# A transformer encoder layer: the first feed-forward product as seven half-size products, its result kept in DRAM, and the second product as a phase of its own

## The chip, the cores and the metric

The kernel runs on one core of one Trainium2 chip. The time is the device time of one execution in microseconds (us); a kernel's time is the median of its runs. One execution of each kernel is also recorded by the hardware profiler, and all durations of single instructions come from that one. The engines are named as in the profile: PE is TensorE (PEld its weight load), DVE VectorE, ACT ScalarE, POOL GpSimd, SP SyncE, which here issues the DMAs.

## The reference

Two inputs, 256 and 1024 tokens of 1024 channels, go through the same encoder layer: a norm, one wide projection, four mixers, a gated merge, an output projection with residual, and a feed-forward part with residual. Cut to the last two, which the change touches:

```python
merged = sum over n of gate[:, :, n] * einsum('blw,wd->bld', branches[n], w_branch[n])
mix_out = einsum('bld,de->ble', merged, w_out)          # 1024 x 1024
x = x + rms_norm(mix_out, norm_mix_post)
h2 = rms_norm(x, norm_ffn_pre)
hidden = square(relu(einsum('bld,df->blf', h2, w_ff1)))  # 1024 x 4096
ff_out = einsum('blf,fd->bld', hidden, w_ff2)            # 4096 x 1024
return x + rms_norm(ff_out, norm_ffn_post)
```

All is float32.

## The kernel before

The 1280 tokens are ten tiles of 128 (`NT`), taken together in chunks of 256, 512 and 512 tokens (`CH`). Every large product is made from three TensorE products: each operand is split into a high part, rounded to the multiplier's float32 form, and a low part that holds the rest, and `PASSES` adds high by high, high by low and low by high in PSUM. Weights come in units of 128 x 512 floats, 256 KB. `wload` loads a unit on SP's queue into one of three raw buffers (L112), casts the high part on ACT (L116) and subtracts it on DVE for the low part (L117); high and low parts lie in a ring of 16 tiles "w".

After the merge, `split` makes the high and low part of a token tile (L973 and L974), the output projection multiplies it with both halves of the output weights, first one half over all of K and then the other (`gemm_b`, L153), and `residual` adds the normed result to the input, stores it, and makes the normed `h2` tile in place of the merged one (L989 to L1002), with two small powers on POOL (L106). `transpose_in` turns each `h2` tile with eight TensorE transposes (L194) into high and low parts (L196 on ACT, L197 on DVE).

In the feed-forward part, `ffn1(f)` makes 128 hidden channels for all tokens: three chunks of 24 matmuls (8 K tiles by 3 passes, `gemm_a`, L146) with 256 or 512 columns, then relu, square and the high part on ACT (L1034 to L1036) and the low part on DVE (L1037). `ffn2(fs)` then multiplies two such hidden blocks with their two weight units and adds the result of every token tile to an accumulator in SBUF (L1058 on TensorE, L1064 on DVE): 15 rounds of 120 to 180 matmuls after a first one. `ffn1` runs up to three hidden blocks ahead. In the last round, `finish` makes the last norm and the output (L1068 to L1090). The order on TensorE from the output projection to `ffn1(0)` is that of the code (`manual_schedule`); elsewhere, and on the other engines, a scheduler sets it from the code's order and the buffers. Each engine works through its own list in order, and an instruction waits for what it reads and for the last use of the buffer that it writes.

## Time and profile before

| | |
|---|---|
| median of 3 runs | 2324.14 us (2323.52 to 2324.39) |
| span of the profiled execution | 2322.2 us |
| from the output projection's first matmul to the first product's | 1307.05 to 1429.24 us |
| feed-forward part | 1429.24 to 2312.64 us (end of the last matmul) |
| after the last matmul | 9.56 us |
| mean granted TensorE clock | 0.997 |

The profiler counts from the first to the last instruction of one execution, so its span is 1.9 us below the median of the runs. Rows of a group read: line, engine, operation, output<-input by the program's names, shapes, count | busy time, mean duration of one in ns | idle time ahead of them and what ended it. A busy TensorE includes overlap of one matmul with the next, so the distance between starts, not the duration of one, tells the pace. Rows of the chain and of a timeline begin with start and duration in us. Rows of a table by stretches give the stretch, its length, the busy time and count of instructions of each engine named (TensorE alone, or TensorE, its weight load, DVE, ACT and POOL), the granted clock, the DMA share and GB/s.

### The profile page before, as it was taken

Reading aid. Unit: us, or ns where it says so; the run is one execution under the profiler, and the core shown is the slowest. Engines: PE = TensorE matmul, PEld = TensorE weight load, DVE = VectorE, ACT = ScalarE, POOL = GpSimd, SP = SyncE. Lnnn points to the kernel's source line nnn. Section 1 sums busy time; section 2 is a strip of 40 time slices with the busy share of each in tenths; the row PEclk is TensorE's granted clock in tenths of the full one; section 3 lists DMA queues with packets and bytes.
Section 4 is the critical chain, followed back from the end, with each engine's and each line's share of the span. In section 5 each row is a group of like instructions: output and inputs, shape, how many; then the busy total and the mean of one; then the engine's idle time right before and its main releaser. Section 6 shows DMA issues by size and latency. Waiting matters only on the chain.

```text
span 2322.2 us, 29598 instructions
## 1 busy us (share of the span) xinstructions
PE 2288.3 (99%) x11680; PEld 1931.8 (83%) x11680; DVE 1084.1 (47%) x1757; ACT 751.8 (32%) x1514; POOL 65.1 (3%) x126
## 2 busy tenths in 40 slices
PE   8999999999999999999999999999999999999998
PEld 6887888878888888888888788888888888888886
DVE  5465599677554332322422455244444444334437
ACT  5333886334332121211211234422222222222223
POOL 1000000000000000000000011000000000000001
PEclk9999999999999999999999999999999999999999
DMA  5212565634276320210211423111111111111104
GB/s 178 77 41 104 177 215 163 200 101 143 87 249 214 120 68 28 82 46 28 96 32 36 137 91 127 37 37 37 37 37 37 37 41 47 40 37 39 43 24 163
DMA packets 117516, 205.22 MB, mean 88 GB/s; under 512 B 11105, under 2 KB 41985, under 8 KB 117377
## 3 DMA queue, kind: packets, MB, share of 16 engines
q1 hardware_dynamic: 107584, 187.60, 25.7%
q10 hardware_dynamic: 9792, 15.73, 1.9%
q8 instruction: 91, 1.49, 0.3%
q14 instruction: 49, 0.39, 0.1%
HBM read 153.40 MB, written 49.89 MB: 88 GB/s over the span
## 4 chain that ended last, share of the span: by engine, by line
PE 92%; DVE 4%; DMA 1%; issue 1%; ACT 1%; POOL 0%; SPq 0%; DVEq 0%; POOLq 0%; ACTq 0%
PE mm L146 47%; PE mm L1058 17%; PE mm L244 11%; PE mm L153 6%; PE mm L251 6%; PE mx L584 1%; DMA raw<-in_wu_dram 1%; DVE acc L1089 1%; PE mx L194 1%; DVE sa L715 0%; DVE acc L1064 0%; PE mx L470 0%; PE mx L595 0%; PE mx L827 0%; PE mx L864 0%
## 5 line engine op out<-in xcount | busy, mean ns | idle before, releaser
L146 PE MATMUL mm<-h2T,whi 128*128 128x512 f32 (+1 forms) x1536 | 408.0, 354 | 0.3 <-ACT h2T L196 0.3
L146 PE MATMUL mm<-hT,whi 128*128 128x256 f32 (+1 forms) x1488 | 395.5, 354 | 0.0
L117 DVE TENSOR_TENSOR wlo<-raw,whi 128x512 fp32r<-128x512 f32 x302 | 206.7, 689 | 373.0 <-ACT whi L116 318.6
L116 ACT CAST whi<-raw 128x512 fp32r<-128x512 f32 x302 | 184.5, 621 | 581.1 <-PE mm L1058 320.5
L146 PEld LDWEIGHTS mm<-h2T,whi 128*128 128x128 f32 x1536 | 271.8, 189 | 40.9 <-ACT h2T L196 0.5
L146 PEld LDWEIGHTS mm<-hT,whi 128*128 128x128 f32 x1488 | 263.4, 189 | 38.9
L1064 DVE TENSOR_TENSOR acc<-acc,mm 128x512 f32<-128x512 f32 x300 | 205.7, 686 | 154.7 <-PE mm L1058 154.7
L146 PE MATMUL mm<-h2T,wlo 128*128 128x512 f32 (+1 forms) x768 | 271.5, 354 | 0.0
L146 PE MATMUL mm<-hT,wlo 128*128 128x256 f32 (+1 forms) x744 | 263.1, 354 | 0.0
L244 PE MATMUL mm<-hT,whi 128*128 128x512 f32 (+1 forms) x960 | 261.4, 360 | 0.0
L1058 PE MATMUL mm<-whi,hidl 128*128 128x512 f32 x640 | 251.1, 392 | 0.0
L1058 PE MATMUL mm<-whi,hidh 128*128 128x512 f32 x640 | 250.2, 391 | 0.0
L1058 PE MATMUL mm<-wlo,hidh 128*128 128x512 f32 x640 | 248.5, 388 | 0.0
L146 PE MATMUL mm<-bt,whi 128*128 128x512 f32 (+1 forms) x768 | 204.3, 354 | 0.0
L244 PEld LDWEIGHTS mm<-hT,whi 128*128 128x128 f32 x960 | 166.9, 189 | 26.4 <-issue 3.3
L244 PE MATMUL mm<-hT,wlo 128*128 128x512 f32 (+1 forms) x480 | 170.2, 355 | 0.0
L1037 DVE TENSOR_TENSOR hidl<-relu,hidh 128x512 fp32r<-128x512 f32 (+1 forms) x96 | 57.9, 603 | 238.8 <-ACT hidh L1036 238.8
L146 PEld LDWEIGHTS mm<-h2T,wlo 128*128 128x128 f32 x768 | 145.1, 189 | 20.2
L146 PEld LDWEIGHTS mm<-hT,wlo 128*128 128x128 f32 x744 | 140.6, 189 | 19.6
L146 PEld LDWEIGHTS mm<-bt,whi 128*128 128x128 f32 x768 | 136.0, 189 | 20.5
L251 PE MATMUL mm<-whi,hT 128*128 128x512 f32 x480 | 151.8, 397 | 0.0
L1058 PEld LDWEIGHTS mm<-whi,hidh 128*128 128x128 f32 x640 | 120.1, 188 | 27.0
(259 smaller groups left out, 2824.0 us busy)
## 6 DMA issues: line engine op xcount, KB each, us to landing
raw<-in_wu_dram SPq DMA_DIRECT2D x310, 256.0 KB, 2.7
E<-acsd SPq DMA_DIRECT2D x20, 512.0 KB, 4.8
bt<-br SPq DMA_DIRECT2D x16, 640.0 KB, 6.1
br<-bo SPq DMA_DIRECT2D x36, 256.0 KB, 3.0
xt<-in_x_dram SPq DMA_DIRECT2D x10, 512.0 KB, 3.8
oxt<-in_x_dram SPq DMA_DIRECT2D x10, 512.0 KB, 3.6
x2d<-oxt SPq DMA_DIRECT2D x10, 512.0 KB, 2.6
fx<-x2d SPq DMA_DIRECT2D x10, 512.0 KB, 3.9
```

Of the source, the lines that this page charges most:

```text
L116: ACT.copy(out=hi, in_=raw)
L117: DVE.tensor_tensor(out=lo, in0=raw, in1=hi.bitcast(F32), op=ALU.subtract)
L146: PE.matmul(ps[:, :n], w.get(a, k), act.rhs(b, k, c), start=j == 0, stop=j == last)
L153: PE.matmul(ps, act.lhs(b, k, t), w.get(a, k), start=j == 0, stop=j == last)
L194: PE.transpose(tp[:, i * 128:(i + 1) * 128], src[:, k, :], ident)
L244: yield from halves(ps, w, n, lambda ps, w, a, b, k, st, sp: PE.matmul(ps[:, :n], w.get(a, k), hT.rhs(b, k, c), start=st, stop=sp))
L251: yield from halves(ps, w, 512, lambda ps, w, a, b, k, st, sp: PE.matmul(ps, hT.lhs(b, k, t), w.get(a, k), start=st, stop=sp))
L584: PE.matmul(yd[:, 64 * h:64 * h + 64], E[:, 128 * h:128 * h + 128], xs[:, 64 * h:64 * h + 64], start=True, stop=True)
L1037: DVE.tensor_tensor(out=hl[:, c0:c0 + n], in0=r[:, :n], in1=hh[:, c0:c0 + n].bitcast(F32), op=ALU.subtract)
L1058: PE.matmul(ps, hid[f][p][:, 128 * t:128 * t + 128], ws[i][e][a], start=j == 0, stop=j == end)
L1064: DVE.tensor_tensor(out=dst, in0=dst, in1=ps, op=ALU.add)
L1089: DVE.scalar_tensor_tensor(out=a, in0=a, scalar=rs, in1=xt[:, cols], op0=ALU.mult, op1=ALU.add)
```

## The change

The first product, `h2` (1280 x 1024) by 1024 x 4096, is cut for each pair of hidden blocks q (256 channels; 16 pairs) into halves in all three directions: the tokens in even and odd tiles (A1x and A2x), K in two halves of 512, the channels in two halves of 128. Seven products of half size take the place of eight, in Winograd's form of Strassen's scheme: `LEFT` lists sums and differences of the token halves, T1 to T4 are differences of weight units, and the four results are sums of the products. P1, P6, P7 and P4 go one after the other into one PSUM bank "a" without a restart, P2 into "c", P5 and P3 into "d". ACT copies the bank out after P1, P6 and P7 (L1157); DVE adds the bank c or d to such a copy and takes relu and square (L1160 to L1175, L1145); P4's result goes through ACT (L1170, L1171). Each product is 12 matmuls (4 K tiles by 3 passes, L1153).

The five pairs of token tiles form a group of two pairs (c = 0, 256 columns) and one of three (c = 1, 384 columns). `build` makes the left operands of one tile pair: 16 transposes (L999), eight operations on ACT and eleven on DVE (L1004 to L1019). The first two pairs are built during the output projection; the other three `h2` pairs are stored to DRAM and read back. There are three phases: for q = 0 to 5 the narrow group alone (with a build after q = 1, 2 and 4), for q = 6 to 15 both groups, and for q = 0 to 5 the wide group alone, with the weights loaded and combined again. So `ff1_w` runs 22 times: four raw loads, four differences (on POOL for the first phase, else on DVE, L1106), seven casts on ACT (L1100) and seven subtractions on DVE (L1101).

The hidden values are stored to DRAM in float32 (L1141) and read back tile by tile in the second product (`load_h`, L1251, with cast and subtraction at L1254 and L1255), which is a phase of its own: eight rounds over K by ten token tiles, each with 24 matmuls of 512 columns (L1277). The accumulator is added to 140 times, not 300. The output projection now takes both halves of the weights at each K tile (L1067), and `split` works on half tiles. The table pools change place, and the code's order on TensorE (`manual_schedule`) now holds to the end.

```diff
+LEFT = ("A11", "A12", "S2", "S1", "S3", "A22", "S4")
+PRODUCTS = (("P1", "A11", "B11", "a"), ("P2", "A12", "B21", "c"), ("P6", "S2", "T2", "a"), ("P5", "S1", "T1", "d"),
+            ("P7", "S3", "T3", "a"), ("P4", "A22", "T4", "a"), ("P3", "S4", "B22", "d"))
+CP = (2, 3)
+HN = (256, 384)
+NQ0 = 6
+BUILD_AT = (1, 2, 4)
...
+    def left(p, c):
+        return {o: [p.tile([128, 4, HN[c]], F32R, name=f"{o}{c}{b}") for b in range(2)] for o in reversed(LEFT)}
+    AL = [left(ap0, 0), None]
+    def ts():
+        return tp.tile([128, 512], F32, tag="ts", name="ts", bufs=3)
 
     def k4(a):
         return a.rearrange("p (k b) -> p k b", b=128)
 
+    def build(p, even, odd):
+        c = 0 if p < CP[0] else 1
+        o = 128 * (p - c * CP[0])
+        def tr(src, g):
+            ps = mx_ps()
+            for i in range(4):
+                PE.transpose(ps[:, i * 128:(i + 1) * 128], src[:, 4 * g + i, :], ident)
+            return ps
+        def put(name, a):
+            hi, lo = (AL[c][name][b][:, :, o:o + 128] for b in range(2))
+            ACT.copy(out=hi, in_=k4(a))
+            DVE.tensor_tensor(out=lo, in0=k4(a), in1=hi.bitcast(F32), op=ALU.subtract)
+        a21, a22, a11, a12 = tr(odd, 0), tr(odd, 1), tr(even, 0), tr(even, 1)
+        x = ts()
+        ACT.copy(out=x, in_=a21)
+        s1 = ts()
+        DVE.tensor_tensor(out=s1, in0=x, in1=a22, op=ALU.add)
+        DVE.tensor_tensor(out=x, in0=a11, in1=x, op=ALU.subtract)
+        put("A22", a22)
+        put("S1", s1)
+        DVE.tensor_tensor(out=s1, in0=s1, in1=a11, op=ALU.subtract)
+        put("A11", a11)
+        put("S3", x)
+        s4 = ts()
+        DVE.tensor_tensor(out=s4, in0=a12, in1=s1, op=ALU.subtract)
+        put("A12", a12)
+        put("S2", s1)
+        put("S4", s4)
...
+        if t >= 2 * CP[0]:
+            SP.dma_start(out=k4(h2d[t]), in_=ht)
...
-        for half in range(2):
-            gemm_b(ps[half], w[half], act, t)
+        for k in range(8):
+            for half in range(2):
+                for i, (a, b) in enumerate(PASSES):
+                    PE.matmul(ps[half], act[k // 4][b][:, k % 4, :], w[half].get(a, k), start=k + i == 0,
+                              stop=k == 7 and i == 2)
         act = nact
         pend.append(residual(t, ps))
-        if 1 <= t <= CT[2][0]:
-            transpose_in(h2T, pend[t - 1], t - 1)
...
+    hid = [dram.tile([NT, 128, 512], F32, name=f"hid{i}") for i in range(DFF // 512)]
...
+    def ff1_w(q, eng):
+        r = {}
+        for name, f, g in (("B11", 0, 0), ("B21", 0, 1), ("B12", 1, 0), ("B22", 1, 1)):
+            if name == "B12":
+                raw = tp.tile([128, 512], F32, tag="raw", name="raw", bufs=1)
+            else:
+                raw = wp.tile([128, 512], F32, tag="raw", name="raw", bufs=3)
+            SP.dma_start(out=raw, in_=wu[FF1_U + 4 * q + 2 * f + g])
+            r[name] = raw
+        out = {}
+        def put(name, a):
+            hi = wp.tile([128, 512], F32R, tag="w", name="whi", bufs=16)
+            lo = wp.tile([128, 512], F32R, tag="w", name="wlo", bufs=16)
+            ACT.copy(out=hi, in_=a)
+            DVE.tensor_tensor(out=lo, in0=a, in1=hi.bitcast(F32), op=ALU.subtract)
+            out[name] = hi, lo
+        def diff(a, b):
+            d = ts()
+            eng.tensor_tensor(out=d, in0=a, in1=b, op=ALU.subtract)
+            return d
+        put("B11", r["B11"])
+        put("B21", r["B21"])
+        t1 = diff(r["B12"], r["B11"])
+        t2 = diff(r["B22"], t1)
+        put("T2", t2)
+        put("T1", t1)
+        t4 = diff(r["B21"], t2)
+        t3 = diff(r["B22"], r["B12"])
+        put("T3", t3)
+        put("T4", t4)
+        put("B22", r["B22"])
+        return out
+    def ff1(q, w, cs, fc):
+        bank = {}
+        tiles = {}
+        def new(c, nm):
+            tiles[c, nm] = fc[c].tile([128, HN[c]], F32, tag=f"fc{c}", name=f"fc{c}", bufs=6 + c)
+            return tiles[c, nm]
+        def ps_of(b, c):
+            if (b, c) not in bank:
+                bank[b, c] = (mm_ps if b == "a" or len(cs) == 1 else mx_ps)()
+                return bank[b, c][:, :HN[c]], True
+            return bank[b, c][:, :HN[c]], False
+        def done(c, nm, half, fo):
+            f = 2 * q + fo
+            dst = hid[f // 4].rearrange("(a b) p c -> b p a c", b=2)[half]
+            o = c * CP[0]
+            SP.dma_start(out=dst[:, o:o + CP[c], 128 * (f % 4):128 * (f % 4) + 128],
+                         in_=tiles[c, nm].rearrange("p (a b) -> p a b", b=128))
+        def relu2(a):
+            DVE.scalar_tensor_tensor(out=a, in0=a, scalar=0.0, in1=a, op0=ALU.max, op1=ALU.mult)
+        for name, lo, ro, b in PRODUCTS:
+            for c in cs:
+                ps, first = ps_of(b, c)
+                j = 0
+                for k in range(4):
+                    for a, p in PASSES:
+                        PE.matmul(ps, w[ro][a][:, 128 * k:128 * k + 128], AL[c][lo][p][:, k, :], start=first and j == 0,
+                                  stop=j == 11, skip_group_check=not first)
+                        j += 1
+                if name in ("P1", "P6", "P7"):
+                    ACT.copy(out=new(c, name), in_=ps)
+                if name == "P2":
+                    s = tiles[c, "P1"]
+                    DVE.tensor_tensor(out=s, in0=s, in1=ps, op=ALU.add)
+                    relu2(s)
+                    done(c, "P1", 0, 0)
+                if name == "P7":
+                    s = tiles[c, "P7"]
+                    DVE.tensor_tensor(out=s, in0=s, in1=bank["d", c][:, :HN[c]], op=ALU.add)
+                    relu2(s)
+                    done(c, "P7", 1, 1)
+                if name == "P4":
+                    s = new(c, "P4")
+                    ACT.activation(out=s, in_=ps, func=AF.Relu)
+                    ACT.activation(out=s, in_=s, func=AF.Square)
+                    done(c, "P4", 1, 0)
+                if name == "P3":
+                    s = tiles[c, "P6"]
+                    DVE.tensor_tensor(out=s, in0=s, in1=ps, op=ALU.add)
+                    relu2(s)
+                    done(c, "P6", 0, 1)
+    NQ = DFF // 256
+    fc = [fc0, None]
+    wq = ff1_w(0, POOL)
+    for q in range(NQ0):
+        nw = ff1_w(q + 1, POOL)
+        ff1(q, wq, (0,), fc)
+        wq = nw
+        if q in BUILD_AT:
+            p = CP[0] + BUILD_AT.index(q)
+            src = []
+            for t in (2 * p, 2 * p + 1):
+                h = hst.tile([128, 8, 128], F32, name="hst", bufs=2)
+                SP.dma_start(out=h, in_=k4(h2d[t]))
+                src.append(h)
+            build(p, *src)
+    hst.release()
+    fc[1] = pool("fc1", side="right")
+    for q in range(NQ0, NQ):
+        nw = ff1_w((q + 1) % NQ, DVE)
+        ff1(q, wq, (0, 1), fc)
+        wq = nw
+    ap0.release()
+    w2p = pool("w2")
+    for q in range(NQ0):
+        nw = ff1_w(q + 1, DVE) if q + 1 < NQ0 else None
+        ff1(q, wq, (1,), fc)
+        wq = nw
...
+    fin = {}
+    units = [0]
+    def ff2_w(kc):
+        ws = {}
+        for e in range(2):
+            for fo in range(4):
+                raw = wp.tile([128, 512], F32, tag="raw", name="raw", bufs=3)
+                SP.dma_start(out=raw, in_=wu[FF2_U + 2 * (4 * kc + fo) + e])
+                pl, tag, nb = (wp, "w", 16) if units[0] % 22 < 8 else (w2p, "w2", 28)
+                units[0] += 1
+                hi = pl.tile([128, 512], F32R, tag=tag, name="whi", bufs=nb)
+                lo = pl.tile([128, 512], F32R, tag=tag, name="wlo", bufs=nb)
+                ACT.copy(out=hi, in_=raw)
+                DVE.tensor_tensor(out=lo, in0=raw, in1=hi.bitcast(F32), op=ALU.subtract)
+                ws[e, fo] = hi, lo
+        return ws
 
...
+    def load_h(kc, t):
+        raw = fp.tile([128, 512], F32, name="hraw", bufs=3)
+        SP.dma_start(out=raw, in_=hid[kc][t])
+        hh = fp.tile([128, 512], F32R, name="hidh", bufs=3)
+        hl = fp.tile([128, 512], F32R, name="hidl", bufs=3)
+        ACT.copy(out=hh, in_=raw)
+        DVE.tensor_tensor(out=hl, in0=raw, in1=hh.bitcast(F32), op=ALU.subtract)
+        return hh, hl
+    NK = DFF // 512
+    kcs = [(i + (NQ0 + 1) // 2) % NK for i in range(NK)]
+    steps = [(i, t) for i in range(NK) for t in range(NT)]
+    ws = ff2_w(kcs[0])
+    nws = None
+    hs = [load_h(kcs[0], 0), load_h(kcs[0], 1)]
+    for n, (i, t) in enumerate(steps):
+        if t == 0 and i:
+            ws = nws
+        if t == 1 and i + 1 < NK:
+            nws = ff2_w(kcs[i + 1])
+        if n + 2 < len(steps):
+            hs.append(load_h(kcs[steps[n + 2][0]], steps[n + 2][1]))
+        h = hs.pop(0)
+        last = i == NK - 1
+        for e in range(2):
+            ps = mm_ps()
+            for fo in range(4):
+                for m, (a, p) in enumerate(PASSES):
+                    PE.matmul(ps, h[p][:, 128 * fo:128 * fo + 128], ws[e, fo][a], start=fo + m == 0,
+                              stop=fo == 3 and m == 2)
...
+    finish(NT - 1)
+    order.close()```

Three places show how the lists of the engines change. In the names, a number behind a tile's name tells one buffer from another; what an instruction waits for stands in brackets.

On ACT in the first product before, the end of one hidden block with the weight casts that follow; `mm` is the PSUM bank of a chunk:

```order
L1034 ACTIVATE relu_13220<-mm_13195 128x512 [waits DVE_49,PE_49]
L1035 ACTIVATE relu_13220<-relu_13220 128x512 [waits Activation_49]
L1036 CAST hidh_13133<-relu_13220 128x512 [waits Activation_49]
L116 CAST whi_13619<-raw_13617 128x512 [waits DMAHW4_49,PE_49]
L116 CAST whi_13625<-raw_13623 128x512 [waits DMAHW5_49,PE_49]
```

On ACT now, in the first phase at q = 1; `mm_12176` is bank a, `fc0` are the copies (P1, P6, P7) and P4's tile, and `whi` are the weights of q = 2: B11, B21, T2, T1, T3, T4 and B22 in this order:

```order
L1157 COPY fc0_12189<-mm_12176 128x256 [waits PE_49]
L1100 CAST whi_12152<-ts_12150 128x512 [waits PE_49,Pool_49]
L1100 CAST whi_12156<-ts_12148 128x512 [waits DVE_49,PE_49]
L1157 COPY fc0_12219<-mm_12176 128x256 [waits PE_49]
L1100 CAST whi_12164<-ts_12162 128x512 [waits PE_49,Pool_49]
L1100 CAST whi_12168<-ts_12160 128x512 [waits DVE_49,PE_49]
L1157 COPY fc0_12246<-mm_12176 128x256 [waits DMAHW7_49,PE_49]
L1100 CAST whi_12172<-raw_12138 128x512 [waits DMAHW5_49,DVE_49,PE_49]
L1170 ACTIVATE fc0_12263<-mm_12176 128x256 [waits DMAHW3_49,DVE_49,PE_49]
L1171 ACTIVATE fc0_12263<-fc0_12263 128x256 [waits Activation_49]
```

Where ACT read a bank once and then worked in SBUF, it now reads the same bank four times, with the casts of the next pair's weights between; the casts of T3 (`whi_12164`) and T4 (`whi_12168`) stand ahead of P7's copy (`fc0_12246`). The ring "w" has eight pairs of high and low tiles for seven operands, so an operand of q = 2 takes the place of the one before it in the list of q = 1: T4 that of T3, which P7 reads.

On DVE now, at the start of the build that follows q = 1; `mx` are the transposed tiles, `ts` the sums, and `A..`, `S..` the left operands:

```order
L1101 TENSOR_TENSOR wlo_12337<-raw_12328,whi_12336 128x512 [waits DMAHW7_49,Activation_49]
L1011 TENSOR_TENSOR ts_12308<-ts_12306,mx_12291 128x512 [waits PE_49,Activation_49]
L1012 TENSOR_TENSOR ts_12306<-mx_12296,ts_12306 128x512 [waits DVE_49,PE_49]
L1005 TENSOR_TENSOR A2211_11921<-mx_12291,A2210_11920 128x4x128 [waits Activation_49]
L1005 TENSOR_TENSOR S111_11925<-ts_12308,S110_11924 128x4x128 [waits DMAHW3_49,DMAHW6_49,DMAHW1_49,Activation_49]
L1005 TENSOR_TENSOR S311_11923<-ts_12306,S310_11922 128x4x128 [waits Activation_49]
L1015 TENSOR_TENSOR ts_12308<-ts_12308,mx_12296 128x512 [waits DVE_49]
L1101 TENSOR_TENSOR wlo_12341<-raw_12330,whi_12340 128x512 [waits DMAHW1_49,PE_49,Activation_49]
```

The build's operations stand among the low parts of the weights of the pair after next; there was nothing of the kind in the first product before.

On SP now, where the first product ends and the second begins; `fc1` are the wide group's hidden tiles, `hraw` the hidden values read back:

```order
L1141 DMA hid2_11909<-fc1_16408 128x3x128 [waits DVE_49]
L1223 DMA raw_16562<-in_wu_dram 128x512 [waits DMAHW6_49,DMAHW2_49,DVE_49]
L1141 DMA hid2_11909<-fc1_16425 128x3x128 [waits Activation_49]
L1214 DMA gfin_16460<-in_rows_dram 128x1024 [waits PE_49]
L1141 DMA hid2_11909<-fc1_16381 128x3x128 [waits DMAHW5_49,DVE_49]
L1251 DMA hraw_16510<-hid3_11910 128x512
L1251 DMA hraw_16516<-hid3_11910 128x512 [waits DMAHW7_49]
```

The store of the last hidden tile (`fc1_16381`, made after P3) waits for DVE, and the loads for the second product, of another 512 channels (`hid3`), stand behind it on the same queue. Before, hidden values never left SBUF and SP had only weights to load here.

124 lines of the change are left out of this document (46 added, 78 removed).

## The prediction

> **What bounds the kernel now.** I read the page first: busy shares, the chain by engine and line, the costly groups.
>
> ```profile
> span 2322.2 us, 29598 instructions
> PE 2288.3 (99%) x11680; PEld 1931.8 (83%) x11680; DVE 1084.1 (47%) x1757; ACT 751.8 (32%) x1514; POOL 65.1 (3%) x126
> PE 92%; DVE 4%; DMA 1%; issue 1%; ACT 1%; POOL 0%; SPq 0%; DVEq 0%; POOLq 0%; ACTq 0%
> raw<-in_wu_dram SPq DMA_DIRECT2D x310, 256.0 KB, 2.7
> ```
>
> TensorE is busy for 99% of the span and makes 92% of the chain; nothing else is above half. The profiled execution spans 2322.2 us and the median of the runs is 2324.1, so I add 1.9 us to a span to compare it with the runs. Next, what TensorE waits for:
>
> ```profile
> PE mm L153 <- ACT wout L116: 4.4, 2, 3.3
> PE mx L194 <- DVE h2T L197: 1.6, 1, 1.6
> PE mm L146 <- ACT h2T L196: 0.3, 1, 0.3
> ```
>
> In the feed-forward part only the last two, 1.9 us together, belong to its start; from there on TensorE never waits. The chain of waits in that part and a table by stretches give the pace:
>
> ```profile
> 1502.40 27.47 PE mm L1058 x120
> 1529.87 27.56 PE mm L146 x144
> 1557.43 27.33 PE mm L1058 x120
> ...
> 1196.07:1198.94 2.87, 2.87 (x25) 1.00 0.28 96
> 1198.94:1209.85 10.91, 10.91 (x51) 1.00 0.15 48
> ```
>
> The pieces alternate: 144 matmuls of the first product (L146, two hidden blocks) and 120 of the second (L1058). The two stretches are one 256-column chunk of 24 matmuls and two 512-column chunks, 48 matmuls (the counts also hold those that straddle an edge). So a 256-column matmul takes 2.87/24 = 119.6 ns, a 512-column one 10.91/48 = 227.3 ns, and 48 x 119.6 + 96 x 227.3 = 27.56 us, just the piece of the chain. The clock column is 1.00. Time can only leave by fewer column-passes, and whatever makes TensorE wait comes on top.
>
> **The change: matmuls.** Before, the first product is 16 pieces of 27.56 = 441.0 us. After, each of 16 column pairs has seven products of 12 matmuls: 84 of 256 columns and 84 of 384. No row has 384 columns. Three quarters of 227.3 is 170.5; one and a half times 119.6 is 179.4; the straight line between both widths gives 173.4, which I take, since both known widths lie on one line with a fixed part of 12 ns. 84 x 119.6 = 10.05 us, 84 x 173.4 = 14.57 us, together 24.6; 16 x 24.6 = 393.8. **Gain 47.2 us** (39 to 51). The second product keeps its 1920 matmuls of 512 columns: 0. Transposes are 80 before and after: 0.  The 1.9 us wait at the start of the first product goes, since the first group's left operands are built six tiles earlier.
>
> **What is added on DVE, ACT and the DMAs.** Prices, by shape, and last two stretches, of 16 transposes and of the whole feed-forward part:
>
> ```profile
> L117 DVE TENSOR_TENSOR wlo<-raw,whi 128x512 fp32r<-128x512 f32 x302 | 206.7, 689 | 373.0 <-ACT whi L116 318.6 <-PE mm L146 37.7 <-PE mm L244 9.4
> L948 DVE SCALAR_TENSOR_TENSOR gth<-gth,mm 128x256 f32<-128x256 f32 x24 | 10.0, 418 | 106.5 <-PE mm L146 106.5
> L1064 DVE TENSOR_TENSOR acc<-acc,mm 128x512 f32<-128x512 f32 x300 | 205.7, 686 | 154.7 <-PE mm L1058 154.7
> L116 ACT CAST whi<-raw 128x512 fp32r<-128x512 f32 x302 | 184.5, 621 | 581.1 <-PE mm L1058 320.5 <-PE mm L146 127.0 <-DMA raw<-in_wu_dram 86.4
> L909 ACT ACTIVATE gth<-mm 128x256 f32<-128x256 f32 x24 | 9.2, 383 | 99.2 <-PE mm L146 98.4 <-issue 0.8
> L648 POOL MEMSET reset<- 128x1280 f32 x1 | 1.2, 1167 | 0.0
> ...
> 1427.58 1.91 PE L194 MATMUL mx<-cst,merged 128*128 128x128 f32 x16
> 1429.24 0.48 PE L146 MATMUL mm<-h2T,whi 128*128 128x256 f32 x2
> ...
> 1427.58:2322.20 894.62, 883.15 (x4257) 744.12 (x4255) 376.32 (x592) 259.70 (x482) 10.30 (x12) 1.00 0.16 49
> ```
>
> One column pair needs on DVE seven subtractions for low parts (7 x 0.69 = 4.8 us) and six 256-wide operations on the hidden tiles (6 x 0.42 = 2.5 us): 7.3 us, against 10.05 us of matmuls in the first phase, where only the 256-column group runs. A pair with a build has 11 more DVE operations (11 x 0.69 = 7.6): 14.9, against 10.05 + 1.7 for its transposes (1429.24 - 1427.58). Over the six pairs of that phase DVE has 6 x 7.3 + 3 x 7.6 = 67 us for 65 of TensorE: level with it, so order decides.
>
> The weight differences run on POOL there, four a pair. The nearest POOL row, one access per element, is 1167/1280 = 0.91 ns; three accesses to 512 elements are 1.4 us, the upper bound; DVE's 0.69 for the same operation the lower. I take 1.2, nearer POOL's own row: 4.8 us a pair beside 10. The Trainium skill, "GPSIMD Engine Reference", section 3.1, puts a two-input operation at about 2.6 cycles an element, by which I estimate 1.1 us; nothing in the sum changes.
>
> The hidden values are 1280 x 4096 x 4 = 21 MB, written once and read once. With the DMAs 16% busy at 49 GB/s there, 42 MB more over 850 us are 49 GB/s more, about a third busy in all: 0, under the matmuls. Not so covered, at the mean rate of the whole span (88 GB/s), they would take 42/0.088 = 477 us; the stores in pieces of 512 bytes have no row here.
>
> **Waits in the first phase.** The fourth product in bank a goes on accumulating P1, P6 and P7, so P4 cannot start until ACT has copied P7 out. In ACT's list the cast of T4 stands ahead of that copy, and this cast overwrites the slot that P7 reads: it cannot start before P7 ends. How fast ACT takes over:
>
> ```profile
> 1281.54 0.28 PE L146 MATMUL mm<-hT,wlo 128*128 128x256 f32 x1
> ...
> 1281.86 0.38 ACT L909 ACTIVATE gth<-mm 128x256 f32<-128x256 f32 x1 [0.22 <-PE mm L146]
> ```
>
> From the last start plus 0.12 us of pace, 1281.66, to 1281.86 are 0.2 us. So TensorE waits 0.2 + 0.6 (cast) + 0.38 (copy) + some 0.05 = **1.2 us** in every pair. In the first pair ACT is also held by the last residual's square, which waits for a POOL result behind the weight differences: P6's copy comes 2.7 us late as well, 3.9 in all. In the three pairs where a build is interleaved, the build's casts and DVE's eleven operations displace the others: P7's copy stands behind a cast that comes 0.8 late, and P3, whose bank DVE must have read, 1.7 late: about 2.5 each. Sum 3.9 + 2 x 1.2 + 3 x 2.5 = **13.8 us**. Bounds: 7 if only the 1.2 remains, 28 if each of the six has twice my figure.
>
> **Second and third phase.** With both groups, P4 of the narrow group (12 x 0.12 = 1.43 us) covers the cast and the wide copy (0.2 + 0.6 + 0.48 + 0.05 = 1.33 us; 0.48 lies between the 0.38 and the 0.62 above): I take 1 us for ten pairs (0 to 5). In the last six pairs only the wide group runs and the cover is gone: 6 x 1.3 = **7.8 us** (4 to 12). Its weights are loaded and combined again, four raw loads of 2.7 us under 14.57 us of matmuls a pair: covered.
>
> **From the first product to the second.** On SP's list the first load of hidden values stands behind the store of the last hidden tile, which waits for DVE's last two operations after TensorE's last matmul. So nothing is prepared: hand-off 0.2, two 384-wide operations 2 x 0.55, issues on SP some 0.4, a 256 KB load 2.7, cast 0.62, low part 0.69: 5.7 us without matmuls. And the clock:
>
> ```profile
> 1321.94 1.65 PE L153 MATMUL mm<-wout,sp 128*128 128x512 f32 x3 [3.32 <-ACT wout L116]
> ...
> 1325.37 0.40 PE L153 MATMUL mm<-wlo,sh 128*128 128x512 f32 x1
> ...
> 1321.94:1324.00 2.06, 2.06 (x5) 1.64 (x6) 0.67 (x1) 0.37 (x1) 0.00 (x0) 0.50 0.29 82
> 1326.00:1330.00 4.00, 4.00 (x19) 3.30 (x19) 2.10 (x3) 1.20 (x3) 0.55 (x1) 1.00 0.32 133
> ```
>
> After a wait of 3.32 us the granted clock is 0.50; eight starts take the 3.43 us up to 1325.37 instead of 8 x 0.227 = 1.82: 1.6 us lost. So the boundary costs 5.7 + 1.6 = **7.3 us** (5 to 10). After the 1.6 us wait at the first product's start the pace was full. What lies between 1.6 and 3.3 us no row shows. I take no drop for the first phase: but for the first pair's 2.7, its waits are pieces of 0.8, 1.2 and 1.7 us, near the 1.6. The Trainium skill, "TensorE: Matmul & The Clock Gate", part 1, lets the clock fall after an idle window of about 3.4 us, and by that rule, too, the boundary alone pays.
>
> **Out projection and tail.** Before, its first tile is held up by loads of its weights:
>
> ```profile
> 1309.48 5.61 DMA raw<-in_wu_dram
> 1316.47 4.78 DMA raw<-in_wu_dram
> 1321.94 13.36 PE mm L153 x51
> ...
> 2312.25 0.39 PE L1058 MATMUL mm<-wlo,hidh 128*128 128x512 f32 x1
> ...
> 2314.26 0.68 DVE acc L1064
> ```
>
> Taking both halves at each K step wants the second half's weights earlier, but they all pass the same three raw buffers, and the tile ends when the last is there: 0 (-2 to +4). In the tail, DVE starts the last add at 2314.26, though the last matmul ends at 2312.25 + 0.39 = 2312.64: it is 1.6 us behind. After the change a step has twelve matmuls a half instead of nine and DVE keeps up: -1.2 (-1.6 to 0). The second product's own operand work per 5.45 us step, some 1.8 casts on ACT (1.1 us) and 1.8 low parts and two adds on DVE (2.6 us), and 1.8 loads, lies beside its matmuls: 0; without that cover it would be 80 x 0.69 = 55 us.
>
> **Sum.** 2322.2 - 47.2 - 1.9 - 1.2 + 13.8 + 1 + 7.8 + 7.3 + 0 = **2301.8 us** span, with 1.9 **2303.7** in the runs. With every unknown term at its lower end it would be 2284, at its upper end 2342; as they hardly all lean one way, I take about two thirds of the way down and half of it up: 2290 to 2322 is the forecast's own range.
>
> **Rivals.**
> *Nearly all of it is kept.* If the hand-offs hide (first phase 7, third 4, boundary 5, second 0), the sum is 2322.2 - 50.3 + 16 = 2288, 2290 in the runs. For it: each wait is little more than one cast and one copy. Against: the order of ACT's list is fixed, and both stand in it behind P7's end.
>
> *DVE sets the first phase.* DVE's 67 us are level with TensorE's 65. At 1.5 times its durations it needs 100, so the phase loses 35 us, not 14: 2325 in the runs; it decides from about 1.2 times on. Against it: 0.69 is a mean with the fixed part, and back to back the operations overlap. Nothing in this trace has POOL and DVE busy together (POOL 3%). The Trainium skill, "GPSIMD Engine Reference", section 8, says the two contend for their memory interfaces when DVE reads two inputs, which is what nearly every DVE operation here does, with POOL busy for half of the phase.
>
> *Slower: the clock falls at the short waits.* If waits of 0.8 to 2.7 us that come back every 10 to 15 us lower the clock as the 3.32 us one did, the ten waits of the first phase and six of the third cost 16 x 1.6 = 25.6 us more: 2329, above the time before. It decides from 13 such drops on. For it: no row has such waits in series. Against it: full pace after 1.6 us.
>
> *The change does not do what it says* (the products not in runs of twelve at full pace): the listing has 84 matmuls for each pair and group, so hardly.
>
> **How the numbers follow.** The forecast 0.62, nearly all kept 0.09, DVE 0.12, the clock 0.13, others 0.04. About 0.2%, 4.6 us, is what can be told from no change here: faster is the forecast, the kept gain and a third of the DVE case, 0.75; the same, half of the DVE case and a third of the clock's, 0.10; slower, the rest of both and of the others, 0.15. The range that holds 8 in 10 goes from 2286, the kept gain with 384 columns at their lower bound, over the DVE case to the clock case's 2329.
>
> **What would show it.** In the changed profile: 12-matmul pieces of 1.43 and 2.08 us; waits of TensorE for ACT's copy at line 1157 near 1.2 us in the first and third phase, and next to none in the second; one gap near 5.7 us at the first matmul of line 1277, released by the cast of the hidden values, with clock 0.5 behind it; DVE near 100% busy in the builds. Wrong would be: granted clock under 0.95 across the first phase, POOL differences over 1.5 us, DVE operations longer than before by a fifth, or a pace of 384 columns above 180 ns.

## The result, and the profile after

The changed kernel takes **2336.15 us** (2334.68 to 2340.75, 4 runs) against 2324.26 us of the kernel before beside it: a ratio of 1.0054 (95% interval 1.004 to 1.0068). It is slower by half a per cent, where 2303.7 us and faster were predicted. Its profiled execution is the longest of the four: 2338.9 us of span (2340.75 us), against a forecast span of 2301.8. The stretches below are those of this execution, 4.6 us longer than the median.

The page of the changed kernel, its busy shares:

```profile
span 2338.9 us, 31256 instructions
PE 2271.2 (97%) x12064; PEld 1959.4 (84%) x12064; DVE 1193.9 (51%) x1968; ACT 774.7 (33%) x1586; POOL 100.1 (4%) x154
```

TensorE is busy 17 us less than before, though by the forecast its two products have 47.2 us of matmuls less (393.8 + 437.3 us against 441.0 + 437.3). And it now waits. The table of TensorE's waits, in the changed parts (engine and line that waits, what it waits for, us in all, times, longest):

```profile
PE mm L1153 <- ACT fc L1157: 18.3, 13, 4.2
PE mm L1153 <- DVE fc L1165: 9.9, 3, 3.3
PE mm L1277 <- ACT hidh L1254: 8.0, 1, 8.0
```

And the table by stretches: output projection, first, second and third phase of the first product, the gap, the second product, the tail (length; busy us and count of PE, PEld, DVE, ACT and POOL; granted clock; DMA share; GB/s):

```profile
1308.73:1428.12 119.39, 116.65 (x512) 93.52 (x513) 74.31 (x121) 51.65 (x106) 17.91 (x23) 1.00 0.43 140
1428.12:1527.68 99.56, 76.88 (x553) 74.30 (x552) 78.77 (x119) 47.97 (x101) 34.04 (x25) 0.90 0.46 137
1527.68:1776.43 248.75, 248.75 (x1682) 248.75 (x1681) 128.83 (x231) 83.17 (x170) 0.00 (x0) 1.00 0.34 96
1776.43:1871.34 94.91, 89.44 (x505) 87.36 (x504) 58.89 (x98) 38.77 (x73) 0.00 (x0) 1.00 0.45 122
1871.34:1879.49 8.15, 0.15 (x2) 0.00 (x1) 2.52 (x6) 1.85 (x3) 0.00 (x0) 0.78 0.88 255
1879.49:2329.43 449.94, 449.89 (x1920) 363.77 (x1920) 204.94 (x326) 103.59 (x189) 4.93 (x9) 1.00 0.32 98
2329.43:2338.90 9.47, 0.00 (x0) 0.00 (x0) 4.70 (x9) 1.45 (x4) 0.55 (x1) 0.70 0.30 111
```

The next table sets the terms of the forecast beside this. The prediction has no times for the single stretches, so the terms are shared out here: the 1.9 us are taken off ahead of the first product, and the transposes of the three builds stand in the first phase.

| stretch | forecast us | measured us | off by |
|---|---|---|---|
| up to the first product | 1427.3 | 1428.1 | +0.8 |
| first phase | 60.3 + 5.0 transposes + 13.8 waits = 79.1 | 99.6 | **+20.5** |
| second phase | 246.2 + 1 = 247.2 | 248.75 | +1.5 |
| third phase | 87.4 + 7.8 = 95.2 | 94.9 | -0.3 |
| gap to the second product | 5.7 | 8.15 | +2.4 |
| second product, with the slow clock at its start | 437.3 + 1.6 = 438.9 | 449.9 | **+11.0** |
| tail | 8.4 | 9.5 | +1.1 |

These add up to the 37 us between the two spans. Two stretches carry most of it.

**The first phase.** TensorE waits for 22.7 us in it, 12.8 for copies on ACT (the other 5.5 of the 18.3 above are in the third phase) and 9.9 for DVE ahead of P3; its instructions take 76.9 us instead of 65.3. The waits for copies in the first phase, DVE's low parts, first in the first phase and then in the second, and POOL's weight differences in the first:

```profile
PE mm L1153 <- ACT fc L1157: 12.8, 7, 4.2
...
L1101 DVE TENSOR_TENSOR wlo<-ts,whi 128x512 fp32r<-128x512 f32 x25 | 20.8, 848 | 5.7 <-ACT whi L1100 5.3
...
L1101 DVE TENSOR_TENSOR wlo<-ts,whi 128x512 fp32r<-128x512 f32 x40 | 27.6, 690 | 46.6 <-ACT whi L1100 46.6
...
L1106 POOL TENSOR_TENSOR ts<-raw,ts 128x512 f32<-128x512 f32 x12 | 17.2, 1429 | 18.0 <-DMA raw<-in_wu_dram 8.3 <-DVE S L1005 5.0 <-DVE wlo L1101 2.6
```

The same subtraction takes 848 ns in the mean beside POOL and 690 without it. A stretch of the timeline in a build shows how (start and duration in us):

```profile
1465.23 1.29 POOL L1106 TENSOR_TENSOR ts<-raw 128x512 f32<-128x512 f32 x1 [10.91 <-DVE S L1005]
1465.67 1.41 DVE L1101 TENSOR_TENSOR wlo<-raw,whi 128x512 fp32r<-128x512 f32 x1
...
1467.00 0.68 DVE L1019 TENSOR_TENSOR ts<-mx,ts 128x512 f32<-128x512 f32 x1
```

A DVE operation that reads two tiles in SBUF and runs into one of POOL's takes 1.41 us and ends 0.56 us after it; those that read one input in PSUM stay at 0.68. The POOL operation itself had waited 10.91 us for the build on DVE. POOL's late differences make the next pair's T3 late, the low part of T3 stands ahead of P7's addition in DVE's list, and P3 waits for this addition because it takes the bank "d" that the addition reads:

```profile
1455.81 0.60 PE L1153 MATMUL mm<-A,whi 128*128 128x256 f32 x2 [2.02 <-ACT fc L1157]
...
1476.25 0.55 PE L1153 MATMUL mm<-S,whi 128*128 128x256 f32 x2 [3.29 <-DVE fc L1165]
...
1455.81:1459.20 3.39, 3.39 (x17) 3.39 (x17) 1.42 (x4) 0.83 (x2) 0.00 (x0) 0.54 0.27 81
1526.15:1529.55 3.40, 3.40 (x27) 1.00 0.77 217
```

The clock falls to about half behind the first pair's wait of 4.23 us, behind two of the three waits of 3.29 us, and here even behind one of 2.02 us (0.54 in the row of 1455.81). Behind the third wait of 3.29 us, which ends at 1526.15, it stays at 1.00 (last row). Over the first phase the granted clock is 0.90; by the starts of the matmuls I estimate that the four falls cost some 8.5 us, so that some 12 of the 20.5 us are waits.

**The second product.** The first and the last of four starts of its matmuls, 512 columns each:

```profile
1900.12 0.40 PE L1277 MATMUL mm<-whi,hidh 128*128 128x512 f32 x1
...
1900.82 0.40 PE L1277 MATMUL mm<-whi,hidh 128*128 128x512 f32 x1
```

The starts are 233.3 ns apart (0.70 / 3), at a clock of 1.00 and with nothing awaited; before it was 27.33 / 120 = 227.8. 1920 x 5.5 ns are 10.6 us of the 11.0.

### The profile page after: what moved, and what is told of

The parts are those of the page before. It is cut to its first block, busy times and chain, and to the rows that moved or that the text cites. A ratio compares the mean times of both kernels' runs of the same rounds, so it can differ in the third digit from the quotient of the medians.

```text
span 2338.9 us, 31256 instructions
## 1 busy us (share of the span) xinstructions
PE 2271.2 (97%) x12064; PEld 1959.4 (84%) x12064; DVE 1193.9 (51%) x1968; ACT 774.7 (33%) x1586; POOL 100.1 (4%) x154
## 5 line engine op out<-in xcount | busy, mean ns | idle before, releaser
L1277 PE MATMUL mm<-whi,hidh 128*128 128x512 f32 x640 | 255.1, 399 | 8.0 <-ACT hidh L1254 8.0
L1277 PE MATMUL mm<-whi,hidl 128*128 128x512 f32 x640 | 254.9, 398 | 0.0
L1277 PE MATMUL mm<-wlo,hidh 128*128 128x512 f32 x640 | 254.8, 398 | 0.0
L128 DVE TENSOR_TENSOR wlo<-raw,whi 128x512 fp32r<-128x512 f32 x174 | 118.4, 688 | 261.3 <-ACT whi L127 207.9
L1283 DVE TENSOR_TENSOR acc<-acc,mm 128x512 f32<-128x512 f32 x140 | 95.8, 685 | 181.5 <-PE mm L1277 181.3
L1153 PE MATMUL mm<-S,whi 128*128 128x384 f32 (+1 forms) x704 | 158.3, 316 | 14.1 <-DVE fc L1165 9.9
L127 ACT CAST whi<-raw 128x512 fp32r<-128x512 f32 x174 | 104.9, 620 | 146.8 <-DMA raw<-in_wu_dram 51.1
L1277 PEld LDWEIGHTS mm<-whi,hidh 128*128 128x128 f32 x640 | 121.3, 190 | 36.6 <-ACT hidh L1254 8.3
L1153 PE MATMUL mm<-A,whi 128*128 128x256 f32 (+1 forms) x608 | 137.6, 317 | 14.0 <-ACT fc L1157 14.0
L1277 PEld LDWEIGHTS mm<-whi,hidl 128*128 128x128 f32 x640 | 121.3, 190 | 29.0 <-DVE hidl L1255 0.4
L1277 PEld LDWEIGHTS mm<-wlo,hidh 128*128 128x128 f32 x640 | 121.2, 189 | 28.5
L920 ACT ACTIVATE gth<-mm 128x512 f32<-128x512 f32 (+1 forms) x72 | 37.9, 526 | 308.5 <-PE mm L157 307.6
```

The source lines that it names most:

```text
L127: ACT.copy(out=hi, in_=raw)
L128: DVE.tensor_tensor(out=lo, in0=raw, in1=hi.bitcast(F32), op=ALU.subtract)
L920: ACT.activation(out=th[:, :n], in_=ps[:, :n], func=AF.Tanh, scale=0.5)
L1153: PE.matmul(ps, w[ro][a][:, 128 * k:128 * k + 128], AL[c][lo][p][:, k, :], start=first and j == 0, stop=j == 11, skip_group_check=not first)
L1277: PE.matmul(ps, h[p][:, 128 * fo:128 * fo + 128], ws[e, fo][a], start=fo + m == 0, stop=fo == 3 and m == 2)
L1283: DVE.tensor_tensor(out=dst, in0=dst, in1=ps, op=ALU.add)
```

## The experiments

In the first phase the theory was that POOL and DVE hold each other up, in the other stretches the waits as forecast. For the second product's pace there was no theory at first. The places of the tiles in SBUF, as the built programs have them, gave one: before, the weights and the activations of nearly every matmul begin at the same remainder (32) modulo 512 bytes of a partition's memory; in the changed kernel the tiles of the right-hand pools do not (96, 224 and 480).

The table has all runs; each ratio is to the kernel before, run beside it on the same chip. The runs were made on several chips, on which the median of the kernel before lay between 2322.3 and 2324.8 us, so a difference of two medians in it is good to 2 us or so:

| run | median us (lowest to highest) | ratio, 95% interval |
|---|---|---|
| the change | 2336.15 (2334.68 to 2340.75) | 1.0054 (1.004 to 1.0068) |
| e1_align | 2335.31 (2335.06 to 2337.27) | 1.0057 (1.0042 to 1.0072) |
| e2_p5late | 2331.38 (2329.82 to 2337.04) | 1.0047 (1.003 to 1.0063) |
| e3_hearly | 2326.85 (2324.80 to 2335.07) | 1.002 (1.001 to 1.0031) |
| e4_buildts | 2327.67 (2324.74 to 2335.39) | 1.0023 (1.0013 to 1.0033) |
| e5_before64 | 2347.51 (2345.86 to 2349.07) | 1.0107 (1.0091 to 1.0122) |
| e7_dvediff | 2315.86 (2314.28 to 2323.18) | 0.9975 (0.9966 to 0.9984) |
| e8_align512 | 2325.13 (2321.67 to 2327.12) | 1.001 (1.0 to 1.002) |
| e9_p3mid | 2315.45 (2312.52 to 2316.11) | 0.9965 (0.9952 to 0.9978) |
| e10_four | 2285.37 (2283.25 to 2287.14) | 0.9829 (0.9815 to 0.9842) |
| e11_five | 2284.91 (2283.42 to 2287.79) | 0.9829 (0.9815 to 0.9842) |
| e12_before448 | 2323.13 (2320.62 to 2325.74) | 0.999 (0.9981 to 0.9999) |

The runs of the changed kernel, and of four of the edits to it, scatter by 6 to 11 us, and the second product's pace differs from profile to profile (below), so differences are read from the stretches of the profiles rather than from the medians.

### Where the operands lie: e1_align, e8_align512, e5_before64, e12_before448

Three unused tiles shift the pools behind them. The diff is that of e1_align, with 16 floats (64 bytes) in each; e8_align512 has 16, 112 and 48 floats in the same three places.

```diff
+    op.tile([128, 16], F32, name="oshift")
     op.release()
     ...
     AL[1] = left(ap1, 1)
+    ap1.tile([128, 16], F32, name="ashift")
     ...
+    fp.tile([128, 16], F32, name="fshift")
     fp.release()
```

> The changed kernel with three unused tiles of 64 bytes a partition, one each among the output projection's operands, the wide group's left operands and the second product's tiles. The order of the instructions is the same; only the addresses of these tiles in SBUF move by 64 bytes, so that both operands of every matmul behind the merge begin at the same remainder modulo 128 bytes (32), where before they were 32 and 96. Theory: the pace of a matmul depends on this; in the changed kernel 512 columns took 233.3 ns a start where the remainders differ and 226.7 in the kernel before where they are equal, 384 columns 176.0 against 173.3. Then 1920 x 6.6 + 480 x 6.6 + 1344 x 2.7 ns = 19.5 us go: about 2317 us, with starts 227 ns apart in the second product. Rival: the pace comes with the new order (twelve matmuls for a bank, operands freshly cast): no change, 2336 us and 233 ns.

Output projection and second product of e1_align, by stretches (TensorE alone), and the first and the last of ten starts in the output projection:

```profile
1308.70:1425.00 116.30, 113.19 (x512) 1.00 0.42 143
1875.26:2323.50 448.24, 448.24 (x1920) 1.00 0.31 98
...
1409.78 0.39 PE L1067 MATMUL mm<-wout,sh 128*128 128x512 f32 x1
...
1411.82 0.39 PE L1067 MATMUL mm<-wlo,sh 128*128 128x512 f32 x1
```

This is a miss, and a telling one. The output projection goes from 119.4 to 116.3 us, with the starts 226.7 ns apart (2.04 / 9); the second product stays at 233.5 ns (448.24 / 1920, with the slow clock at its start). After the shift the output projection's operands lie at 32 and 32 modulo 512, but the second product's at 32 and 160, and the wide group's at 416 and 32: alike modulo 128 only. So being alike modulo 128 is not enough.

> The changed kernel with unused tiles of 64, 448 and 192 bytes a partition, so that both operands of every matmul behind the merge begin at remainder 32 modulo 512 bytes; with 64 bytes each (the run before) only the output projection had that, and only it got faster (226.7 ns a start). Theory (one remainder modulo 512): second product at 227 ns a start, wide group at 173.3: 3 us less in the output projection, 3.6 in the first product and 4 to 13 in the second (whose pace was 229 or 233 ns in one and the same kernel): 2318 to 2325 us, and the runs lie closer together. Rival (another cause in the second product): 2333 us, as with the 64 bytes.

Second and third phase and second product of e8_align512:

```profile
1526.10:1772.10 246.00, 246.00 (x1683) 1.00 0.33 97
1772.10:1866.60 94.50, 89.05 (x505) 1.00 0.44 122
1874.16:2311.50 437.34, 437.32 (x1920) 1.00 0.32 101
```

With one remainder modulo 512 the second product takes 437.3 us: 227.8 ns a matmul with the slow start in it, and 12.6 us less than in the profile of the change. The second phase takes 246.0 us, which is what the forecast had for its matmuls alone. The theory stands, with the median of 2325.1 us at the upper end of its range; the rival gave 2333 us. That the runs would lie closer together did not come true: they span 5.5 us, those of the change 6.1. Whether 256 would do in place of 512 is not shown, since no run has long matmuls whose operands are alike modulo 256 and not modulo 512.

```diff
     hp = pool("h8")
+    sh64 = pool("shift")
+    sh64.tile([128, 16], F32, name="shift")
     wp = pool("w")
```

> The kernel before with one unused tile of 64 bytes a partition between the pool of the activations and that of the weights, and nothing else. Where the activations and the weights of a matmul both began at remainder 32 modulo 512 bytes, the weights now begin at 96. Theory (the pace depends on whether both operands have one remainder modulo 512): some 5900 matmuls of 512 columns take 6.6 ns more each, as in the output projection of the changed kernel (233.3 against 226.7), so 25 to 40 us more: about 2350 to 2363 us, most of it ahead of the feed-forward part's end and none in matmuls of 256 columns. Rival (the pace belongs to the changed kernel's code): no change, 2322 to 2324 us.

Groups of matmuls in the kernel before, then in e5_before64 (`bt` are operands of the merge, ahead of the changed parts):

```profile
L146 PE MATMUL mm<-h2T,whi 128*128 128x512 f32 x1024 | 316.3, 390 | 0.3 <-ACT h2T L196 0.3
L146 PE MATMUL mm<-bt,whi 128*128 128x512 f32 x512 | 158.4, 391 | 0.0
L1058 PE MATMUL mm<-whi,hidl 128*128 128x512 f32 x640 | 251.1, 392 | 0.0
L1058 PE MATMUL mm<-wlo,hidh 128*128 128x512 f32 x640 | 248.5, 388 | 0.0
```

```profile
L148 PE MATMUL mm<-h2T,whi 128*128 128x512 f32 x1024 | 322.0, 395 | 0.3 <-ACT h2T L198 0.3
L148 PE MATMUL mm<-bt,whi 128*128 128x512 f32 x512 | 158.4, 391 | 0.0
L1060 PE MATMUL mm<-wlo,hidh 128*128 128x512 f32 x640 | 252.1, 394 | 0.0
```

64 unused bytes in front of the weights cost the kernel before 25 us, just below the range expected, with the same instructions. The matmuls of the first product, whose operands now lie at 32 and 96, take 395 ns instead of 390 (a lone one's duration; it includes the overlap). In pace this is some 3 ns for each, not the 6.6 of the theory: a piece of 144 matmuls takes 27.85 us instead of 27.56, and 96 of them have 512 columns. Those of `bt` do not change: there the shift moves both operands, from 32 and 32 to 96 and 96. So the effect belongs to the place of the operands and not to the changed kernel's code, and it is the distance of the two that counts.

In the kernel before, only the hidden values of two blocks in three lay at another remainder (480). One tile more there:

```diff
+    qp.tile([128, 112], F32, name="qshift")
     qp.release()
```

> The kernel before with one unused tile of 448 bytes a partition among the hidden values of two blocks in three, whose remainder modulo 512 was 480 against 32 of the weights. Theory: 1280 matmuls of 512 columns go from 228.9 to 226.7 ns a start: 2.8 us less, about 2320 us against 2322.5. Rival: no change.

In e12_before448 the three groups of the second product read alike:

```profile
L1058 PE MATMUL mm<-whi,hidl 128*128 128x512 f32 x640 | 249.0, 389 | 0.0
```

392 ns became 389, and the median is 0.1% less, with an interval that just excludes no change: 1.6 us rather than 2.8.

### What makes TensorE wait between the products: e2_p5late, e9_p3mid

First the order of the seven products, given here by their names alone; the weights are built in the same order, and P7's addition comes after P5:

```diff
-PRODUCTS = P1 P2 P6 P5 P7 P4 P3
+PRODUCTS = P1 P2 P6 P7 P5 P4 P3
```

> The changed kernel with P5 moved behind P7, so that 12 matmuls stand between P7 and P4 while the copy of P7 is made; the weights are prepared in that order too. Theory: TensorE waits for that copy since P4 goes on in the same bank; the six waits of 1.07 us in the third phase go, and in the first phase those of 1.1 to 2.2 us: together 6 + 9, about 2321 us. Rival: in the first phase DVE and POOL set the time, so the wait only moves on to P3 there: 6 us less alone, about 2330 us.

First and third phase of e2_p5late, and a wait in the third:

```profile
1427.80:1523.50 95.70, 76.20 (x554) 0.89 0.45 139
1772.20:1867.10 94.90, 89.43 (x505) 1.00 0.43 121
...
1795.37 0.62 PE L1153 MATMUL mm<-S,whi 128*128 128x384 f32 x2 [0.91 <-ACT fc L1157]
```

Neither theory came true: the third phase is as long as before, to a tenth of a microsecond. That the median is near the rival's 2330 us is luck: what is saved lies in the first phase (3.9 us), and in this profile the second product ran at a better pace (441.7 us). The wait of 0.91 us now stands ahead of P7, a product of the S operands, and no longer ahead of P4 (A22): with P5 moved, P6 and P7 are neighbours in bank a, and P7 waits for the copy of P6 as P4 had waited for the copy of P7. The edit moved the wait; it did not test the cause. The next one does: in the first and third phase P3 comes between P7 and P4, in a bank of its own, so that the copy of P7 has a product to run beside.

```diff
+PRODUCTS1 = P1 P2 P6 P5 P7 P3 P4
...
+                if name == "P5" and len(cs) == 1:
+                    s = tiles[c, "P6"]
+                    DVE.tensor_tensor(out=s, in0=s, in1=ps, op=ALU.add)
```

> The changed kernel with P3 ahead of P4 and in a bank of its own in the first and third phase (one DVE addition more for each channel pair), so that no two neighbouring products go into bank a any more. Theory: the waits of 1.07 us in the third phase were the copy out of bank a between two products of it (P7 and P4, and P6 and P7 when P5 was moved, which left the third phase at 94.9 us); now the third phase is 94.9 - 6.4 = 88.5 us, and the first phase loses the waits ahead of P4 (1.1 to 2.2 us each), 5 us or so: about 2325 us. Rival: ACT's list as such is too full there and the wait shows up ahead of another product: 94.9 us again, 2334 us.

First and third phase of e9_p3mid, and all its waits for copies out of bank a:

```profile
1429.30:1515.40 86.10, 72.33 (x553) 0.94 0.49 150
1764.20:1853.20 89.00, 89.00 (x505) 1.00 0.44 127
...
PE mm L1158 <- ACT fc L1162: 11.9, 7, 4.3
```

The third phase has no wait left: TensorE is busy for all of its 89.0 us. The first goes from 99.6 to 86.1, more than expected, but not for the reason given: the waits for copies there only go from 12.8 to 11.9 us. What is gone are the 9.9 us ahead of P3, which has a bank of its own now and no longer waits for P7's addition, though POOL still makes the differences; with them went some of the falls of the clock (0.94 against 0.90). The median drops by 20.7 us to 2315.5, below the kernel before. Of the 24.7 us between the two profiles, 7.1 are the second product's pace, which was the better of two in this one (442.84 us).

### What the first phase waits for: e4_buildts, e7_dvediff

In e4_buildts the sums of the builds get two buffers of their own, in place of those that the weight differences use; in e7_dvediff DVE makes the weight differences in place of POOL.

```diff
-        x = ts()
+        x = tmp()
...
-            build(p, *src)
+            build(p, *src, tmp=lambda: hst.tile([128, 512], F32, tag="bt", name="bt", bufs=2))
```

> The changed kernel with two buffers of their own for the sums in the three builds of the first phase, which otherwise share three buffers with the weight differences on POOL. Theory: POOL's differences for the next pair wait until the build has given the shared buffers back, which makes T3 and P3 late (3.45 us three times, and the clock falls behind it); with own buffers these waits are under 2 us and the clock stays at 1.00: 9 to 12 us less, about 2326 us. Rival: DVE has more work in these pairs than TensorE, whatever the buffers: the same waits, 2334 to 2337 us.

First phase and second product of e4_buildts, and its waits for P7's addition:

```profile
1427.30:1520.40 93.10, 75.59 (x554) 72.33 (x554) 77.14 (x118) 48.02 (x101) 33.36 (x26) 0.91 0.47 146
1872.20:2313.80 441.60, 441.58 (x1920) 361.65 (x1920) 203.99 (x324) 103.49 (x189) 4.79 (x9) 1.00 0.31 99
...
PE mm L1153 <- DVE fc L1165: 2.0, 2, 1.0
```

The waits of P3 are nearly gone (9.9 us in three before, 2.0 in two here), and the first phase is 6.5 us shorter, so the shared buffers were a cause. But at 93.1 us it is far from 79, and the clock is still at 0.91. The rest of the gain between the two profiles is again the second product at its better pace, 441.6 us, with the same addresses and order of matmuls there as in the change, so it is in part luck that the median meets the 2326 us expected.

```diff
-    wq = ff1_w(0, POOL)
+    wq = ff1_w(0, DVE)
...
-        nw = ff1_w(q + 1, POOL)
+        nw = ff1_w(q + 1, DVE)
```

> The changed kernel with the 28 weight differences of the first phase on DVE, where the later phases have them, and none on POOL. Theory: in the first phase POOL and DVE hold each other up; a low part on DVE takes 848 ns there and 690 in the second phase, a difference on POOL 1.42 us. Without POOL the low parts are back at 690 ns and T3 is ready earlier, so the waits for P3 shrink from 3.4 to about 2 us and the clock does not fall behind them: the first phase from 99.6 to about 92 us, 2328 us in all. Rival (DVE's amount of work sets the phase): 25 operations of 0.69 us more on DVE against 14 us of stretching saved: 3 us more or no change, 2335 to 2339 us.

First phase of e7_dvediff, and the low parts on DVE in it:

```profile
1428.80:1509.40 80.60, 69.57 (x554) 66.49 (x553) 74.51 (x137) 46.83 (x99) 1.72 (x2) 1.00 0.52 165
...
L1101 DVE TENSOR_TENSOR wlo<-ts,whi 128x512 fp32r<-128x512 f32 x22 | 15.0, 687 | 1.3 <-ACT whi L1100 1.3
```

The rival falls. DVE makes 23 differences itself in this stretch, 137 operations in all instead of 119, and is yet busy for 74.5 us instead of 78.8, because none of them is stretched: 687 ns instead of 848. The first phase takes 80.6 us, less than the theory's 92, the clock stays at 1.00, the first pair's wait is 1.9 us instead of 4.2, and the median is 20.3 us less. This one edit puts the phase within 1.5 us of the forecast. What it does not separate are three things that go together: DVE's operations are not stretched, a difference takes 0.69 us in place of 1.43, and with one engine for builds and differences the shared buffers hold nothing up (e11_five, below).

### The gap ahead of the second product: e3_hearly

```diff
+        if q == NQ0 - 1:
+            for t in range(2):
+                raw = ts()
+                SP.dma_start(out=raw, in_=hid[(NQ0 + 1) // 2][t])
+                early.append(raw)
         ff1(q, wq, (1,), fc)
```

> The changed kernel with the first two loads of hidden values issued ahead of the last channel pair's products, into the buffers that the weight differences no longer use. Theory: the 8.2 us gap at the start of the second product is the store, load and cast chain behind the last product, and the clock falls behind it; the load no longer belongs to it, so the gap is under 1.5 us and the clock stays at 1.00: 8 to 9 us less, about 2327.5 us. Rival: the weights of the second product are late as well, and the gap shrinks by only 2 to 3 us: about 2333 us.

The waits of e3_hearly at the second product:

```profile
PE mm L1286 <- ACT hidh L1263: 1.1, 1, 1.1
PE mm L1286 <- DVE hidl L1264: 0.8, 1, 0.8
```

8.0 us became 1.9, and the median is 9.3 us less, as expected. In the profiles, both with the second product at its slower pace, the spans differ by 5.6 us only, so part of the 9.3 belongs to something else. The clock was at 0.90 in the 17 us behind the waits: it fell to half behind these 1.9 us, so a fall of the clock was not avoided altogether. The weights were not late.

### All of it: e10_four, e11_five

e10_four has four edits together, those of e8_align512, e9_p3mid, e7_dvediff and e3_hearly; e11_five has that of e4_buildts besides.

> The changed kernel with four of the edits together: operands of one remainder modulo 512 bytes, P3 ahead of P4 in a bank of its own, the two early loads of hidden values, and the weight differences of the first phase on DVE. Theory: four separate causes, so their gains add up, but for the first phase, where two of them meet: 19 us there (99.6 to about 78), 3 in the second phase, 7 in the third, 8 at the start of the second product, 13 in the second product at most, 3 in the output projection: about 2285 us, 1.6% less than the kernel before. Rival: they cover each other (DVE, with the differences, one addition more and the builds, becomes the bound of the first phase): 2295 us or more.

> As e10_four, with the buffers of their own for the sums of the builds too. Theory: with the differences on DVE itself, which works in order, nothing waits for these buffers any more: the same within 3 us, about 2285 us. Rival: the builds still hold the next pair's differences up: another 5 us less, 2280 us.

The three phases, the gap and the second product of e10_four:

```profile
1428.80:1501.00 72.20, 67.36 (x554) 1.00 0.57 174
1501.00:1746.90 245.90, 245.90 (x1682) 1.00 0.35 102
1746.90:1834.30 87.40, 87.40 (x506) 1.00 0.46 135
1834.30:1836.64 2.34, 0.17 (x1) 1.00 0.86 224
1836.64:2274.00 437.36, 437.29 (x1920) 1.00 0.33 103
```

The median is 2285.4 us, 1.7% less than the kernel before and 2.2% less than the change as it came, as expected. By stretches the gains are 27.4 us in the first phase, 2.9, 7.5 and 5.8 in the next three rows and 12.6 in the second product. In the first phase they overlap (19.0 and 13.5 us for the two edits alone), as the theory had it; the four medians alone would promise 61 us, and together they give 50.8. The buffers of their own (e11_five) add nothing once DVE makes the differences, as expected. The third phase is 6 x 84 matmuls of 173.4 ns without a wait.

## Why the prediction was wrong

- **The matmuls, a gain of 47.2 us.** This was right in what the products need: with operands at one remainder, the second phase takes 245.9 us and the third 87.4, to the tenth what 119.6 and 173.4 ns give. In the change, the wide group ran some 3 ns slower (second phase 248.75), for the reason below.
- **The second product at 0.** This step failed. "Keeps its 1920 matmuls of 512 columns" was true, but not at 227.8 ns: 10.6 us too few. The pace was taken as a property of the width. What the runs show in its place is the distance of the operands: with these at one remainder the product takes the 437.3 us of the forecast (e8_align512). The profile of before had a hint: groups of equal matmuls with means of 388 and 392 ns at L1058.
- **The waits of the first phase, 13.8 us.** This step failed most: the phase took 20.5 us more than forecast, some 12 of them waits and some 8.5 the clock. The mechanisms named were there: P4 behind P7's copy (1.2 forecast, 1.0 to 2.0 measured), the first pair held by the residual (3.9 forecast, 4.2 and 0.8 measured), P3 behind DVE in the builds (1.7 forecast, 3.3 measured three times). The 2.7, 0.8 and 1.7 us in them were read from the order of the lists and stand in no row. What was missing is that POOL and DVE stretch each other, and that the builds and POOL's differences share three buffers. The forecast took DVE's operations at the price that they have alone, and POOL's at 1.2 us (measured 1.3 in the median, up to 1.85, and 1.43 in the mean, just past its upper bound of 1.4). Each of three edits takes more than half of P3's 9.9 us away: with buffers of their own for the builds 2.0 are left, with DVE in place of POOL 4.3, and with a bank of its own for P3 none. How much the stretching costs by itself is not separated.
- **The rival "DVE sets the first phase"** had one cause, at a chance of 0.12, but not the mechanism. It put the point from which it decides at 1.2 times DVE's durations, and 848 / 690 = 1.23 was measured. But the phase lost 34 us with DVE busy for 78.8 of 99.6, where the rival gave 35 with DVE busy for 100: that the two losses agree is luck. DVE's amount of work did not set the phase, for e7_dvediff gave DVE more operations and made it shorter. The Trainium skill's "GPSIMD Engine Reference", section 8, which stood beside it, says that the two contend when DVE reads two SBUF inputs; the trace agrees, with 1.41 us for such an operation beside POOL and 0.68 for one that reads PSUM.
- **The clock.** The forecast took no fall in the first phase. It fell behind the waits of 4.23 us and two of 3.29, as the row of before would have it, and behind one of 2.02, so the rival "the clock falls at the short waits" was partly right: not behind each of 16, but behind four. The Trainium skill's "TensorE: Matmul & The Clock Gate", part 1, speaks of an idle window of about 3.4 us; the 2.02 us wait here is shorter than that, and the measurement decides.
- **Second and third phase.** There is no wait in the second (1 us forecast). In the third there are six of 0.91 us. Between e8_align512, which has them, and e10_four, which has not, at one placing of the operands, the phase goes from 94.5 to 87.4 us: 7.1 us, against 7.8 forecast. Cover and lack of cover were read rightly from the order.
- **The gap, 5.7 us.** The mechanism was right, the size short by 2.4: the load took 5.2 us, not 2.7. The gain row had gone out 2 us before the first of three loads of hidden values, three loads of weights followed, and the DMAs were 88% busy; that this is why it took so long was not tested.
- **Output projection and tail.** The first product began 0.8 us later than forecast; a slower pace of 3.1 us in the projection (e1_align) stood against 32 transposes in it, where before it was 64. In the tail nothing was gained: 9.5 us against 9.6 before.

So the sum's gain in the first product was right and its losses were short by 37 us. Two terms make 31 of them: the first phase, where a rival with too small a chance had part of the cause, and the second product's pace, of which no rival had thought.

## What to carry to other kernels

A matmul's pace is a property of where its two operands lie as well as of its width: when pools are moved or a small tile is added, look at the distance between starts in the matmuls whose code did not change. Work moved to an idle POOL isn't free if DVE reads two SBUF tiles beside it; count what it does to DVE before counting what it takes off it. A product that accumulates on a bank which another engine must first copy needs another product between the two, and an edit that swaps neighbours may only move such a wait. After an edit that worked, look whether the waits that it was made for are the ones that went.
